# Split weights for the keys' projection, and matmul passes given first choice, in a two-layer hybrid decoder step

## The chip, the cores and the metric

The kernel runs on one core of a Trainium2 chip. The metric is the device time of one execution in microseconds (us); lower is better. Before the change the median of three runs is 1530.75 us (1529.62 to 1531.14). One execution was profiled: it took 1529.38 us, of which the profile's span covers 1527.6 us.

A core has five engines that run side by side, each through its own queue in order: TensorE (matrix products; the profile shows its matmuls as PE and its weight loads as PEld), VectorE (DVE), ScalarE (ACT), GpSimd (POOL) and SyncE (SP), which here issues the transfers. TensorE multiplies a stored 128x128 block of weights with a moving operand and adds up in a PSUM bank; there are eight banks.

## The reference

One step of a decoder trunk with two layers and 1024 features, for 256 prompt tokens and 8 sequences of 4 sample tokens, 288 columns in all. All of it is float32. Each layer adds half a SwiGLU block, a mixer, half a second SwiGLU block and a gated projection. The mixer is Mamba-2 in layer 0 and RWKV-7 in layer 1. The change concerns RWKV, cut here to what matters:

```python
u_prev = jnp.concatenate([shift0[:, None].astype(u.dtype), u[:, :-1]], axis=1)
xx = u_prev - u
mixed = u[None] + xx[None] * mu[:, None, None, :]
xr, xw, xk, xv, xa, xg = ...
r = xr @ w_r
k = xk @ w_k
v = xv @ w_v
w = -jax.nn.softplus(-(w0 + jnp.tanh(xw @ w1) @ w2)) - 0.5
a = jax.nn.sigmoid(a0 + (xa @ a1) @ a2)
g = jax.nn.sigmoid(xg @ g1) @ g2
...
S = (S * d_t[:, :, None, :] + sa[..., None] * (kk_t * a_t)[:, :, None, :]
     + v_t[..., None] * k_t[:, :, None, :])
```

w_r, w_k, w_v and the output matrix are 1024x1024: 8 by 8 tiles of 128x128.

## The kernel before, in words

Activations stand with features on the 128 partitions and the 288 tokens along the row, so a 1024-feature tensor is eight tiles of 128x288. The kernel runs eight stages in order: feed-forward, Mamba, feed-forward, gate of layer 0; feed-forward, RWKV, feed-forward, gate of layer 1.

**Products in three passes.** Most matrix products split both operands into a rounded high part, in a reduced float32 format that TensorE takes in one pass (fp32r in the profile), and a low part, the rest. `mm3` (L156) then issues three matmuls for each weight tile: high weights by high activations, high weights by low activations, low weights by high activations. All of them go through `mm` (L147), so in the profile they carry line L149. `hilo` (L162) splits an activation: a copy on ScalarE (L141) and a subtraction on VectorE (L167 or L170).

**Two streams of weights.** `Stream` loads units of eight weight tiles (512 KB) on SyncE's queue (L42). `ws` carries the weights that are split: for each four tiles ScalarE writes the high part whi (L57) and VectorE the low part wlo (L58). It splits up to 16 tiles ahead of use; its units have four buffers (`wraw`), the split parts six. `wn` carries weights used whole, in plain float32 (`next_whole`): in RWKV the first matrices of decay, a and gate (r_wa1, r_g1: 8 and 16 tiles) and w_k (64 tiles). Its first unit is loaded before the stage, into a buffer of `wraw`; when the stage begins, `k.wn.pool, k.wn.bufs = pool, 2` gives the later ones two buffers of their own (L1521). A plain float32 tile stands in the profile as two matmuls and two weight loads with raw as the weight.

**The RWKV stage.** `lead` (L1059) normalises, makes xx, mixes the gate's input and forms the sums of r_wa1 and r_g1 (the gate's sums stay in banks 2 and 3 until `gates` reads them). Then the main loop runs over p, one 128-feature block of outputs (two heads) at a time, and interleaves three things that belong to different blocks: `chain(p-2)`, the recurrence of a block, a series of small matmuls that each wait for VectorE or ScalarE and give them work in turn (solve, solved, state, then the group norm); `prep`, which makes the matrices of a block in two halves that run in two loops (it reads k, r, sw and sa, inverts triangular blocks in half precision, and uses banks 2, 3 and 7); and `fill(p)`, the projections. `fill` runs `bulk2(p-1)` (gate output g and the v projection) and `bulk(p+1)` (k and r, and `small`: the decay sw and the rate sa, one split tile each, then a sigmoid on VectorE at L1133 and on ScalarE). The projections use banks 0 and 1 in turn. In `bulk`, for p = 0 the order is k, small, r; for the later blocks it is small, k, r. Each projection is eight weight tiles, after each of which the generator hands back, so that the loop can set 1.6 of them against each step of the others. `mix` (L1115) makes xk, xv, xr with the first block: xk stays whole, xv and xr are split by `hilo`. For the last block the order of all matmuls is fixed by hand (`kept`), and in the last two loops the output matrix takes the projections' place.

**What sets the order.** The source gives a program order. A scheduler then plays all engines through in simulated time: whenever an engine is free, it issues the ready instruction that stands first, by its priority, which is its place in the program order unless the source says otherwise. So a projection's passes fill the times in which the small matmuls of `chain` and `prep` aren't ready, pass by pass if need be. The order found is fixed; on the chip each engine follows its list.

## Time and profile before

| | us |
|---|---|
| median of 3 runs | 1530.75 |
| the profiled execution | 1529.38 |
| its span | 1527.6 |
| TensorE busy: matmuls, weight loads | 1504.1, 1418.5 |
| VectorE, ScalarE busy | 1099.2, 966.1 |
| the L149 matmuls with high weights and act (5520) | 1121.7 |
| the L149 matmuls with plain weights (176 for 88 tiles) | 54.0 |
| all splits of weights: ScalarE, VectorE (754 each) | 473.5, 515.8 |

A matmul's record needs care: the next matmul starts while the record of the last is still open, so a mean duration (297 ns for a split pass) is longer than the step from start to start. The times of a stretch are therefore read from start to start. PEld is the weight loads' own row. A window gives busy times in a stretch of the span; the chain of waits follows the last instruction back to whatever released it.

### The profile page before, as it was taken

The numbers are of one execution on the slowest core, as the hardware profiler recorded it, in microseconds if no ns is written. First come the engines' busy times: TensorE is split into PE (matmuls) and PEld (weight loads), VectorE is DVE, ScalarE is ACT, GpSimd is POOL, SyncE is SP. The second block draws the span as 40 slices with busy tenths as digits, with TensorE's granted clock in tenths as the row PEclk, the third lists the DMA queues.
The fourth block names the chain that finished last, engine by engine and source line by source line (L and its number), as shares of the span: only waits on it lengthen the run. The fifth ranks groups of instructions, "written<-read, shape, count | busy, mean of one in ns | idle before, by whom it ended". The sixth has DMA issues, their size and how long they took to land.

```text
span 1527.6 us, 35589 instructions
## 1 busy us (share of the span) xinstructions
PE 1504.1 (98%) x14178; PEld 1418.5 (93%) x14178; DVE 1099.2 (72%) x2320; ACT 966.1 (63%) x2201; POOL 60.2 (4%) x162
## 2 busy tenths in 40 slices
PE   9999999999999999999999999999999999999997
PEld 9999998999999999999999999777777778999997
DVE  7666578899998666656876655897777768666666
ACT  6555458999997655554755554586666646555545
POOL 0000002112110000000000000200000000000000
PEclk9999999999999999999999999999999999999999
DMA  7555564766766555555555555622221125555552
GB/s 233 166 167 165 167 204 138 241 235 214 240 220 195 174 167 167 165 169 166 170 166 166 166 166 166 208 84 73 71 85 58 62 75 165 167 167 166 166 169 68
DMA packets 75575, 243.48 MB, mean 159 GB/s; under 512 B 11728, under 2 KB 16976, under 8 KB 75408
## 3 DMA queue, kind: packets, MB, share of 16 engines
q1 hardware_dynamic: 75408, 241.21, 49.1%
q8 instruction: 111, 1.82, 0.5%
q14 instruction: 56, 0.46, 0.1%
HBM read 226.54 MB, written 14.64 MB: 158 GB/s over the span
## 4 chain that ended last, share of the span: by engine, by line
PE 91%; DVE 4%; ACT 3%; DMA 1%; issue 1%; SPq 0%; DVEq 0%; ACTq 0%
PE bank L149 85%; PE bank L783 1%; DVE wlo L58 1%; PE bank L787 1%; PE bank L779 1%; DMA raw<-in_wn 1%; ACT whi L57 1%; PE bank L760 0%; DVE AA L1288 0%; ACT L136 0%; PE bank L818 0%; ACT seg L141 0%; DMA raw<-in_w 0%; PE bank L752 0%; ACT xc L141 0%
## 5 line engine op out<-in xcount | busy, mean ns | idle before, releaser
L149 PE MATMUL bank<-act,whi 128*128 128x288 f32 x5520 | 1121.7, 297 | 2.5 <-ACT whi L57 1.6
L149 PEld LDWEIGHTS bank<-act,whi 128*128 128x128 f32 x5520 | 885.7, 188 | 11.0 <-ACT whi L57 2.1
L149 PE MATMUL bank<-act,wlo 128*128 128x288 f32 x2760 | 812.4, 295 | 0.1
L57 ACT ACTIVATE whi<-raw 128x512 fp32r<-128x512 f32 x754 | 473.5, 632 | 445.6 <-PE bank L149 435.3
L58 DVE TENSOR_TENSOR wlo<-raw,whi 128x512 fp32r<-128x512 f32 x754 | 515.8, 689 | 270.2 <-ACT whi L57 241.9
L149 PEld LDWEIGHTS bank<-act,wlo 128*128 128x128 f32 x2760 | 520.4, 189 | 1.9 <-DVE wlo L58 0.3
L149 PE MATMUL bank<-more,whi 128*128 128x288 f32 x384 | 77.1, 295 | 0.0
L149 PEld LDWEIGHTS bank<-more,whi 128*128 128x128 f32 x384 | 61.4, 188 | 0.0
L149 PE MATMUL bank<-act,raw 128*128 128x288 f32 x176 | 54.0, 429 | 2.7 <-DVE sw L1133 1.4
L335 DVE TENSOR_TENSOR u<-bank,s 128x288 f32<-128x288 f32 x88 | 40.2, 456 | 22.8 <-PE bank L149 22.8
L149 PE MATMUL bank<-more,wlo 128*128 128x288 f32 x192 | 56.4, 294 | 0.0
L332 DVE TENSOR_TENSOR t<-bank,rstd 128x288 f32<-128x288 f32 x88 | 39.8, 456 | 22.2 <-PE bank L149 22.1
L684 DVE SCALAR_TENSOR_TENSOR conv_a<-X,vec,conv_a 128x312 f32<-128x312 f32 x96 | 51.0, 535 | 2.4 <-ACT conv_a L141 2.1
L141 ACT ACTIVATE s<-t 128x288 f32<-128x288 f32 x104 | 45.8, 443 | 6.1 <-DVE t L377 4.4
L141 ACT ACTIVATE X<-bank 128x256 f32<-128x256 f32 (+2 forms) x98 | 30.6, 343 | 16.9 <-PE bank L149 16.2
L149 PEld LDWEIGHTS bank<-act,raw 128*128 128x128 f32 x176 | 29.9, 189 | 11.2 <-DVE sw L1133 1.7
L141 ACT ACTIVATE act<-h,vec 128x288 fp32r<-128x288 f32 (+1 forms) x71 | 37.0, 527 | 4.1 <-DMA h<-in_xT 2.9
L149 PEld LDWEIGHTS bank<-more,wlo 128*128 128x128 f32 x192 | 36.2, 189 | 0.0
L136 ACT ACT_TABLE_LOAD x25 | 32.1, 1283 | 1.1 <-PEq L1761 0.7
L170 DVE SCALAR_TENSOR_TENSOR act<-h,vec,act 128x288 fp32r<-128x288 f32 x56 | 28.3, 512 | 5.6 <-ACT act L141 5.6
L181 DVE TENSOR_TENSOR ss<-ss,sq 128x288 f32<-128x288 f32 x62 | 28.0, 452 | 1.9 <-ACT sq L141 1.7
L141 ACT ACTIVATE sq<-h 128x288 f32<-128x288 f32 x63 | 26.9, 431 | 3.8 <-DVE h L381 3.7
(371 smaller groups left out, 1605.4 us busy)
## 6 DMA issues: line engine op xcount, KB each, us to landing
raw<-in_w SPq DMA_DIRECT2D x377, 512.0 KB, 3.6
h0a<-in_ssm_a SPq DMA_DIRECT2D x16, 512.0 KB, 5.8
h0b<-in_ssm_b SPq DMA_DIRECT2D x16, 512.0 KB, 5.4
out_ssm_s<-h0b SPq DMA_DIRECT2D x16, 512.0 KB, 4.4
raw<-in_wn SPq DMA_DIRECT2D x11, 512.0 KB, 4.2
S<-in_wkv_in SPq DMA_DIRECT2D x8, 256.0 KB, 3.0
out_wkv_s<-S SPq DMA_DIRECT2D x8, 256.0 KB, 2.1
h<-in_xT SPq DMA_DIRECT2D x8, 144.0 KB, 4.5
```

Of the source, the lines that this page charges most:

```text
L57: nc.scalar.activation(hi, src, AF.Copy)
L58: nc.vector.tensor_tensor(lo, src, hi.bitcast(F32), ALU.subtract)
L136: load = self.nc.scalar.preload_act_table_set(s)
L141: i = self.nc.scalar.activation(out, in_, func, **kw)
L149: i = self.nc.tensor.matmul(*a, **kw)
L170: nc.vector.scalar_tensor_tensor(lo, src, scale, hi.bitcast(F32), ALU.mult, ALU.subtract)
L181: nc.vector.tensor_tensor(self.ss, self.ss, sq, ALU.add)
L332: nc.vector.tensor_tensor(t, pg, r, ALU.mult)
L335: nc.vector.tensor_tensor(u, pu, s, ALU.mult)
L684: nc.vector.scalar_tensor_tensor(a[:, :312], X[:, t:t + 312], k.g(f"conv_w{t}")[:, ct:ct + 1], a[:, :312], ALU.mult, ALU.add)
L779: nc.tensor.matmul(pyi[q:q + 32, 128 + 4 * b:132 + 4 * b], h0a[:, b, q:q + 32], C[:, 256 + 4 * b:260 + 4 * b], start=True, stop=True)
L783: nc.tensor.matmul(py[64 * hh:64 * hh + 64, o:o + n], xdt[:n, c, 2 * j + hh], Pm[:n, hh, o:o + n], start=True, stop=True)
```

## The change

Four things are edited.

1. `mm3` issues its second and third pass inside `high_priority`, which gives them the priority of the program's start: once such a pass is ready, it goes ahead of everything else that is ready on TensorE. This holds for all stages. With `follow`, the first pass gets it as well.
2. `proj` sets `follow` for the blocks after the first (p > 0), for all tiles but the first of each four (kt % 4 > 0). So four weight tiles, twelve passes, come one after another once the first pass of the first has been issued, as far as they are ready.
3. The keys' projection goes through `mm3` too. Its 64 weight tiles move from `wn` to `ws` (288 and 24 tiles in place of 224 and 88) and are split; xk is split by `hilo` into the tiles 0 to 7 and eight new tiles xkl.
4. `small` runs between k and r for every block, not ahead of k for the later ones, and the two buffers of `wn`'s own are gone: its units after the first go to the four of `wraw`.

```diff
+    def together(self, follow):
+
+        return self.tc.high_priority() if follow else contextlib.nullcontext()
+
-    def mm3(self, ps, w, x, start, stop):
+    def mm3(self, ps, w, x, start, stop, follow=False):
         (wh, wl), (xh, xl) = w, x
-        self.mm(ps, wh, xh, start=start, stop=False)
-        self.mm(ps, wh, xl, start=False, stop=False)
-        self.mm(ps, wl, xh, start=False, stop=stop)
+        with self.together(follow):
+            self.mm(ps, wh, xh, start=start, stop=False)
+        with self.together(True):
+            self.mm(ps, wh, xl, start=False, stop=False)
+            self.mm(ps, wl, xh, start=False, stop=stop)
...
             if i == 0:
                 out[kt] = k.A[8 + kt], k.A[16 + kt]
+            elif i == 2:
+                out[kt] = k.A[kt], self.t(f"xkl{kt}", dt=F32R)
...
             if p == 0:
                 self.mix(i, kt, x)
-            if n == "k":
-                self.k.mm(ps, k.wn.next_whole("r_wk", kt, p), x[kt], start=kt == 0, stop=kt == KD - 1)
-            else:
-                k.mm3(ps, k.ws.next("r_w" + n, kt, p), x[kt], kt == 0, kt == KD - 1)
+            k.mm3(ps, k.ws.next("r_w" + n, kt, p), x[kt], kt == 0, kt == KD - 1, p > 0 and kt % 4 > 0)
...
-            k.renew(0, 8, F32)
-            k.renew(8, 16)
-            self.xk = k.A[0:8]
-            self.xv, self.xr = [[None] * KD for _ in range(2)]
+            k.renew(0, 16)
+            self.xk, self.xv, self.xr = [[None] * KD for _ in range(3)]
...
-        if p > 0:
-            yield from small()
         yield from self.proj("k", 2, self.xk, p)
-        if p == 0:
-            yield from small()
+        yield from small()
         yield from self.proj("r", 0, self.xr, p)
...
-        k.wn.pool, k.wn.bufs = pool, 2
...
-COUNT = {"ffn": 24 * KF, "ple": 80, "mamba": 520, "rwkv": 224}
-WHOLE = {"rwkv": 88}
+COUNT = {"ffn": 24 * KF, "ple": 80, "mamba": 520, "rwkv": 288}
+WHOLE = {"rwkv": 24}
```

## The prediction

> **What bounds the kernel now.** I read the page first, for the share of each engine, then the table of windows, then the chain that ended last.

> ```profile
> span 1527.6 us, 35589 instructions
> ...
> PE 1504.1 (98%) x14178; PEld 1418.5 (93%) x14178; DVE 1099.2 (72%) x2320; ACT 966.1 (63%) x2201; POOL 60.2 (4%) x162
> ...
> PEld   9999998999999999999999999777777778999997
> ```

> TensorE is the engine to ask about, and its weight loads show a dent only in slices 26 to 33, which is the RWKV stage (about 970 to 1270 us). Two windows, one of a feed-forward stage and one of an RWKV loop (start and end, length, then busy time and count of PE, PEld, DVE, ACT, POOL, the granted clock, the DMA share and GB/s):

> ```profile
> 1300.00:1350.00 50.00, 50.00 (x380) 50.00 (x380) 32.53 (x58) 26.29 (x48) 0.00 (x0) 1.00 0.52 167
> ...
> 1112.08:1143.76 31.68, 31.35 (x495) 23.65 (x493) 23.49 (x66) 21.47 (x60) 0.00 (x0) 1.00 0.27 81
> ```

> The feed-forward stage runs 380 passes in 50 us, 0.131 us each, with nothing between: a new order of passes can win nothing there, and the same holds for the gates. What the change is worth is read in the RWKV loop. Its chain:

> ```profile
> by line: PE bank L149 90.0%; DVE AA L1288 5.7%; DVE wlo L58 1.9%; DVE sa L1133 1.6%; DVE sw L1133 0.9%; DVE S L1446 0.9%; issue 0.9%
> ...
> 1142.22 0.30 DVE sw L1133
> ...
> 1142.65 0.51 DVE sa L1133
> 1143.16 0.60 DVE wlo L58
> 1143.76 0.60 DVE AA L1288
> ```

> ```profile
> 1080.40 1.21 DVE AA L1288 x2
> ...
> 1206.95 1.25 DVE AA L1288 x2
> ```

> The pair of AA masks comes back every 31.6 us (four loops from 1080.40 to 1206.95). In a loop TensorE carries the chain for nine tenths; once per loop it passes to VectorE for 2 to 3 us, where sw, sa and a weight split stand ahead of the masks.

> **The loop, part by part.** How projections and small matmuls alternate, from TensorE's timeline:

> ```profile
> 1062.03 0.31 PE L149 MATMUL bank<-Z,XT 64*64 64x64 f16 x8
> 1062.17 0.29 PE L149 MATMUL bank<-XT,Z 64*64 64x64 f16 x8
> 1062.39 0.75 PE L149 MATMUL bank<-act,raw 128*128 128x288 f32 x2
> ...
> 1114.71 0.75 PE L149 MATMUL bank<-act,raw 128*128 128x288 f32 x2
> 1115.39 0.33 PE L149 MATMUL bank<-rhs,TT 64*64 64x64 f32 x4
> ...
> 1125.74 1.24 PE L149 MATMUL bank<-act,raw 128*128 128x288 f32 x4
> 1126.91 0.33 PE L149 MATMUL bank<-rhs,TT 64*64 64x64 f32 x4
> 1127.17 0.54 PE L149 MATMUL bank<-act,whi 128*128 128x288 f32 x2
> 1127.54 0.29 PE L149 MATMUL bank<-act,wlo 128*128 128x288 f32 x1
> 1127.77 0.33 PE L149 MATMUL bank<-SAV,BKt 128*64 128x64 f32 x2
> ...
> 1142.15 0.29 PE L149 MATMUL bank<-la,wlo 128*128 128x288 f32 x1
> ```

> Start to start, a plain float32 tile (two instructions) that stands alone takes 1115.39 - 1114.71 = 0.68, a pair of them 1126.91 - 1125.74 = 1.17. A tile in three split passes that stands alone takes 1127.77 - 1127.17 = 0.60, against 3 x 0.131 = 0.39 in a long run: each run of passes pays 0.21 for its two ends. The small matmuls pay as well: eight of them take 0.14 when more small ones follow (1062.03 to 1062.17), 0.22 when a projection follows (1062.17 to 1062.39), so about 0.1 per change.

> From 1114.71 to 1142.15 the loop holds 20 runs of projection tiles: 16 plain instructions for k in six runs (four tiles alone, two pairs: 4 x 0.68 + 2 x 1.17 = 5.06) and 57 split passes (24 for v, 24 for r, 9 for g, sw and sa) in 14 runs, 9.6 us start to start by the rows between these two.

> - *k in three passes, two groups of four.* Two runs of 12 passes: 2 x (12 x 0.131 + 0.21) = 3.57 for 5.06, saved 1.5. Without grouping, eight lone tiles save only 8 x 0.08 = 0.6.
> - *v and r in groups.* 57 passes in about 6 runs: 57 x 0.131 + 6 x 0.21 = 8.7 for 9.6, saved 0.9.
> - *Fewer changes.* The small matmuls stand in 18 stretches; with these runs and the normalisations' pairs left, about 11: 7 x 0.1 = 0.7 saved.
> - *sw and sa between k and r instead of ahead of k.* They leave the VectorE stretch of the chain (0.30 + 0.51 above). The split and the masks stay: 0.8 saved. They write single buffers that the running preparation reads; later in the loop that read is longer past, so I add no wait.

> That is 3.9 us. Against it stands what the scattered tiles do now: they fill TensorE's waits for VectorE in the dependent steps. Where such a wait is bare already:

> ```profile
> PEld bank L149 <- DVE TT L1381: 3.2, 4, 0.8
> PEld bank L149 <- DVE rhs L1426: 3.0, 9, 0.7
> ```

> Seven stretches lose their filler. A bare wait costs 0.33 (3.0 over 9, the solve steps) to 0.8 (3.2 over 4), and nothing where the other two of the three interleaved sequences have matmuls ready: 0 to 5.6 us. I take half of the seven at 0.33, the row of the solve steps, which stand beside k and r: 1.2. Net 2.7 per loop, bounds -1.7 (slower) to 3.9. Six loops carry a k projection (outputs 2 to 7; 0 and 1 fall in the opening): 6 x 2.7 = 16.2. The two loops after them have v alone; half of the 0.9 + 0.7 each makes 1.6, of which I take 1, since the last steps have an order of their own. Feed-forward, Mamba and gate stages: 0, within 1 either way.

> The splits of k's weights are new work beside this: 8 tiles in a loop are two splits.

> ```profile
> L57 ACT ACTIVATE whi<-raw 128x512 fp32r<-128x512 f32 x754 | 473.5, 632 | 445.6 <-PE bank L149 435.3
> ...
> L58 DVE TENSOR_TENSOR wlo<-raw,whi 128x512 fp32r<-128x512 f32 x754 | 515.8, 689 | 270.2 <-ACT whi L57 241.9
> ...
> raw<-in_wn SPq DMA_DIRECT2D x11, 512.0 KB, 4.2
> ```

> ScalarE goes from 21.5 to 22.7 us in a loop, VectorE from 23.5 to 24.9. A loop of 29 us hides both; one of 25 would not. The weights are the same bytes on the same queue.

> **The opening, which pays.** Between the lead and the first loops VectorE is the bound:

> ```profile
> 970.00:1010.00 40.00, 35.30 (x220) 26.28 (x219) 38.02 (x99) 28.82 (x81) 10.26 (x35) 1.00 0.50 163
> ```

> ```profile
> L167 DVE TENSOR_TENSOR act<-t,act 128x288 fp32r<-128x288 f32 x8 | 3.4, 448 | 0.2 <-ACT act L141 0.2
> L58 DVE TENSOR_TENSOR wlo<-raw,whi 128x512 fp32r<-128x512 f32 x5 | 3.4, 683 | 0.1
> ```

> Splitting xk adds 8 x 0.45 = 3.6 to VectorE, and the weights of the first two k projections up to 4 x 0.68 = 2.7, so 3.6 to 6.3 with no cover (VectorE 38.0 of 40). ScalarE's share has room. Second, the gate's weights (in_wn) no longer get two buffers of their own but queue for the four that the main stream uses. SyncE, then TensorE and VectorE in that time:

> ```profile
> 974.17 0.33 SPq L42 DMA_DIRECT2D raw<-in_wn  x1
> 974.92 0.33 SPq L42 DMA_DIRECT2D raw<-in_w  x1
> 975.31 0.42 SPq L42 DMA_DIRECT2D raw<-in_wn  x1
> ...
> 988.63 0.33 SPq L42 DMA_DIRECT2D raw<-in_w  x1
> ```

> ```profile
> 981.38 5.98 PE L149 MATMUL bank<-act,raw 128*128 128x288 f32 x24
> 988.01 4.15 PE L149 MATMUL bank<-act,raw 128*128 128x288 f32 x16 [0.65 <-DMA raw<-in_wn]
> ...
> 998.53 0.29 PE L149 MATMUL bank<-ql,ones_m 128*128 128x288 f32 x1
> ```

> ```profile
> 987.88 0.68 DVE L58 TENSOR_TENSOR wlo<-raw,whi 128x512 fp32r<-128x512 f32 x1
> ```

> The load at 974.92 takes the buffer that the first gate unit leaves; the next buffer comes free with the split that ends at 988.56, and the load follows at 988.63. In the changed kernel the second unit of gate weights stands at that place and lands 4.2 later, at 993. The third needs one more unit split, which needs passes of k done: after eight mixes and half of their splits, about 996.5, landed at 1000.7. Its eight tiles take 16 x 0.248 = 4.0 (4.15 less the last 0.43, over 15), to 1004.7, where the last gate matmul now ends at 987.4. Behind it waits the first preparation, whose norm goes into a bank that the gate's sum holds: done about 1006 where it is now at 998.8, so 7 late. On SyncE a load that waits holds up what is queued behind it, here the constants and the states; they are needed only after that norm, so I price nothing for them. VectorE has its 3.6 to 6.3 to do in that time, so the two are not added: 7, bounds 3.6 (the loads come in time) and 10 (part of the VectorE work comes after the wait).

> **Sum.** -16.2 - 1 + 7 = -10.2. The profiled execution took 1529.38 (span 1527.6), so 1519.2; the median of the runs, 1530.75, lies 1.4 above it, so 1520.5.

> **Rivals.** *Slower: the dependent steps set the loop's length.* PEld is busy for 23.65 of 31.68 us, no more than VectorE with 23.49, so TensorE may be held by waits that short fillers happen to cover. A run of 12 passes is 1.78 long where a tile alone is 0.60 or 0.68; a step that comes ready just behind its start is up to 1.1 later, six times a loop, and the seven bare waits follow. From 3.9 us of these the loop gains nothing (seven waits at 0.56, between the two rows), and the opening's 7 us remain: 1537.8; with waits at 0.8 it is 10 us more. Against it speaks the chain, nine tenths TensorE, with PE idle for 0.33 us. [...] Chance 0.24.

> *The order hardly groups.* The priorities only act where an instruction is ready when its engine is free in the planned order; if splits come late there, the tiles stay scattered. Then a loop gains 8 x 0.08 for k and half of sw and sa's 0.8, 1.0, six loops 6, against 7: 1531.8, no change. Chance 0.13.

> *All of it.* The waits stay covered (3.9 a loop) and the opening costs VectorE's 3.6 alone: -23.4 - 1 + 3.6 = -20.8, 1510. Chance 0.17.

> **How the numbers follow.** My forecast has 0.46; between net gains of 1.6 and 3.4 per loop and 4 to 10 us of opening it reaches from 1513 to 1530, nearly all of it below 1527.7. A difference under 0.2%, 3 us, can't be told from none here. Faster: 0.46 + 0.17 = 0.63. Same: 0.13. Slower: 0.24. The range leaves out the slower half of the first rival (0.12) and less than half of the last (0.07): 1509 to 1538.

> **What would show it.** Right: the AA pair returns every 28 to 30 us; whi and wlo rows of 12 passes without small matmuls between; PE idle per loop up from 0.33 to about 1.5; VectorE near 25 a loop; the last gate matmul near 1004 and the first ql norm near 1006. Wrong: a period of 31 us or more with TensorE waiting for rhs, SAV or Z (first rival); passes still three by three (second); gate weights issued before 985 (the opening is cheaper); or a feed-forward window with fewer than 378 passes in 50 us, which no step here foresees.

## The result and the profile after

The changed kernel takes 1565.45 us (median of four runs, 1563.89 to 1566.72) where the kernel before takes 1530.86 beside it: a ratio of 1.0227 (95% interval 1.0209 to 1.0245), 34.6 us slower. The forecast was 1520.5 with a range up to 1538. The profiled execution took 1563.89.

The page of the changed kernel, with lines moved by one (L150 is the matmul, L58 and L59 the splits of weights):

```profile
span 1562.1 us, 35769 instructions
...
PE 1518.1 (97%) x14242; PEld 1444.5 (92%) x14242; DVE 1113.4 (71%) x2344; ACT 979.3 (63%) x2225; POOL 60.5 (4%) x162
...
PEclk9999999999999999999999999879999879999999
```

The same row on the page of before:

```profile
PEclk9999999999999999999999999999999999999999
```

Two things stand there. TensorE's rows are busy for 14 us more while the span grew by 34.5, so it is idle for 44.0 us where it was idle for 23.5. And the granted clock, nine tenths or more in every slice before, falls below nine tenths in two places of the RWKV stage.

For what follows I cut the stage into four parts, by the same marks in every kernel: from the first plain matmul of the lead to the first AA masks (the opening), two loops, five steady loops, and the last part up to the last group norm. First before, then after (columns as in the prediction's windows):

```profile
969.60:1007.31 37.71, 33.63 (x188) 24.74 (x188) 35.72 (x92) 26.55 (x75) 10.26 (x35) 1.00 0.49 157
1007.31:1048.08 40.77, 39.59 (x639) 32.03 (x640) 34.05 (x93) 31.60 (x82) 0.00 (x0) 1.00 0.24 84
1048.08:1206.91 158.83, 157.33 (x2440) 119.50 (x2439) 118.98 (x329) 109.35 (x302) 0.00 (x0) 1.00 0.24 72
1206.91:1272.95 66.04, 62.01 (x872) 48.62 (x868) 43.86 (x117) 32.32 (x87) 0.00 (x0) 0.97 0.24 74
```

```profile
968.21:1014.15 45.94, 39.66 (x221) 30.55 (x223) 40.99 (x104) 32.44 (x87) 9.85 (x35) 0.89 0.35 110
1014.15:1067.19 53.04, 48.72 (x660) 40.86 (x658) 37.63 (x98) 35.52 (x90) 0.00 (x0) 0.81 0.22 70
1067.19:1234.19 167.00, 155.39 (x2463) 127.59 (x2460) 125.96 (x338) 114.16 (x308) 0.00 (x0) 0.94 0.24 76
1234.19:1307.19 73.00, 63.52 (x859) 51.23 (x860) 43.14 (x116) 31.10 (x85) 0.00 (x0) 0.85 0.18 59
```

All four parts are longer: 8.2, 12.3, 8.2 and 7.0 us, 35.7 together. What lies behind them is the same (254.6 us before, 254.9 after), and the feed-forward window still holds 380 passes:

```profile
1335.00:1385.00 50.00, 50.00 (x380) 50.00 (x379) 32.39 (x58) 26.27 (x49) 0.00 (x0) 1.00 0.53 169
```

The last column but two is the clock. Length times what it lacks to 1.00, summed over the parts, is 36.1 us after (5.1, 10.1, 10.0, 11.0) and 2.0 before: 34 us more. Length less PE busy, the idle time, is 31.7 after and 10.8 before: 21 more. The two make 55 and the parts grew by 35.7, so at most some 19 us of TensorE's work went away (an estimate, and an upper one: what the clock lacks is taken as lost wholly; two pairs of kernels below lost two thirds to nine tenths of it). That is the kind of work the forecast wanted to save, and more than twice as much was lost in its place.

Where the loops lose it shows in TensorE's timeline of one steady loop (start, length of the stretch, operation; in brackets idle time and who ended it):

```profile
1149.98 0.33 PE L150 MATMUL bank<-rhs,TT 64*64 64x64 f32 x4
...
1152.78 1.10 PE L150 MATMUL bank<-AR,S 64*64 64x8 f32 x32
1153.82 0.40 PE L150 MATMUL bank<-ch,ones_m 128*128 128x288 f32 x1
1155.18 0.40 PE L150 MATMUL bank<-cl,ones_m 128*128 128x288 f32 x1 [0.96 <-DVE cl L1217]
...
1156.17 0.33 PE L150 MATMUL bank<-SAV,AA 64*64 64x64 f32 x4 [0.23 <-ACT s L142]
...
1157.28 0.68 PE L150 MATMUL bank<-act,whi 128*128 128x288 f32 x2
...
1158.00 0.68 PE L150 MATMUL bank<-act,whi 128*128 128x288 f32 x2
...
1160.77 0.43 PE L150 MATMUL bank<-act,whi 128*128 128x288 f32 x2
...
1161.16 0.42 PE L150 MATMUL bank<-act,whi 128*128 128x288 f32 x2
```

From 1148 on TensorE runs dependent steps, with only the small projections' passes (gate and decay) between them and no projection tile of v, k or r. It waits 0.96 for VectorE with nothing to put there. Then the tiles come, all at once, in groups of twelve passes, but a tile now takes 0.72 (1157.28 to 1158.00), where it takes 0.39 once the clock is full again (1160.77 to 1161.16). In windows of two microseconds:

```profile
1150.00:1152.00 2.00, 1.80 (x31) 1.39 (x30) 1.49 (x6) 1.43 (x6) 0.00 (x0) 1.00 0.34 131
1152.00:1154.00 2.00, 1.99 (x36) 1.57 (x36) 1.36 (x6) 1.88 (x7) 0.00 (x0) 1.00 0.49 128
1154.00:1156.00 2.00, 0.98 (x3) 0.37 (x2) 2.00 (x6) 1.11 (x3) 0.00 (x0) 1.00 0.09 32
1156.00:1158.00 2.00, 1.83 (x10) 1.76 (x11) 1.24 (x4) 1.94 (x6) 0.00 (x0) 0.63 0.00 0
1158.00:1160.00 2.00, 2.00 (x9) 1.77 (x8) 0.91 (x2) 0.90 (x4) 0.00 (x0) 0.52 0.00 0
...
1030.00:1032.00 2.00, 1.14 (x22) 0.86 (x18) 1.50 (x4) 1.83 (x5) 0.00 (x0) 1.00 0.05 12
1032.00:1034.00 2.00, 1.58 (x17) 1.02 (x11) 2.00 (x7) 0.83 (x2) 0.00 (x0) 0.91 0.00 0
...
1042.00:1044.00 2.00, 2.00 (x29) 1.54 (x26) 0.00 (x0) 1.10 (x3) 0.00 (x0) 0.50 0.00 0
...
1050.00:1052.00 2.00, 2.00 (x14) 1.83 (x16) 1.04 (x2) 1.05 (x4) 0.00 (x0) 0.83 0.10 41
```

TensorE is idle for 1.02 of two microseconds (1154 to 1156), and the clock granted next is one half, for 3.41 us from 1156.51. In the second loop it is idle for 0.86 and 0.42 of two (1030 to 1034), and the clock is one half for 17.07 us from 1033.63. In this stage the changed kernel has ten stretches at half clock: five of 3.41 us, one of 6.83, three of 10.24 and one of 17.07. TensorE's single waits are shorter than any of these: none between 1150 and 1156 is longer than 0.97 and none in the stage longer than 1.5, and in the 3.41 us ahead of 1156.51 PE is busy for 2.22.

Idle time isn't the whole of it either. The kernel before halves its clock once in this stage, from 1227.36 to 1230.77, and by its records PE is busy for 6.77 of the 6.83 us ahead of that, with small matmuls and projections mixed:

```profile
1221.00:1226.00 5.00, 4.95 (x89) 3.79 (x88) 2.95 (x9) 2.56 (x10) 0.00 (x0) 1.00 0.67 214
1226.00:1231.00 5.00, 5.00 (x65) 3.92 (x60) 1.84 (x5) 2.94 (x7) 0.00 (x0) 0.66 0.02 6
```

And behind 998.66 to 1002.08, where PE is busy for only 2.00 of 3.42 us, the kernel before keeps its 1.00. So scattered idle time stands ahead of most drops here (in the changed kernel 0.51 to 1.88 us of the 3.41 ahead of nine of the ten, 0.21 ahead of the tenth, at 1187.23); that it is what brings them is not shown.

### The profile page after: what moved, and what is told of

It is laid out like the page before. It is cut to its first block, busy times and chain, and to the rows that moved or that the text cites. A ratio compares the mean times of both kernels' runs of the same rounds, so it can differ in the third digit from the quotient of the medians.

```text
span 1562.1 us, 35769 instructions
## 1 busy us (share of the span) xinstructions
PE 1518.1 (97%) x14242; PEld 1444.5 (92%) x14242; DVE 1113.4 (71%) x2344; ACT 979.3 (63%) x2225; POOL 60.5 (4%) x162
## 4 chain that ended last, share of the span: by engine, by line
PE 87%; DVE 6%; ACT 5%; issue 1%; DMA 1%; POOL 0%; SPq 0%; DVEq 0%; ACTq 0%
PE bank L150 82%; ACT whi L58 1%; DVE wlo L59 1%; PE bank L790 1%; PE bank L786 1%; PE bank L794 1%; ACT seg L142 1%; PE bank L767 0%; ACT s L142 0%; ACT sa L142 0%; PE bank L759 0%; DMA raw<-in_w 0%; ACT X L142 0%; DMA raw<-in_wn 0%; ACT ch L142 0%
## 5 line engine op out<-in xcount | busy, mean ns | idle before, releaser
L150 PE MATMUL bank<-act,whi 128*128 128x288 f32 x5584 | 1144.9, 299 | 7.4 <-ACT act L142 2.8
L150 PEld LDWEIGHTS bank<-act,whi 128*128 128x128 f32 x5584 | 904.4, 190 | 18.8 <-ACT act L142 4.4
L150 PE MATMUL bank<-act,wlo 128*128 128x288 f32 x2824 | 833.4, 296 | 0.1
L58 ACT ACTIVATE whi<-raw 128x512 fp32r<-128x512 f32 x770 | 483.0, 632 | 459.3 <-PE bank L150 447.6
L59 DVE TENSOR_TENSOR wlo<-raw,whi 128x512 fp32r<-128x512 f32 x770 | 526.2, 689 | 282.7 <-ACT whi L58 257.4
L150 PEld LDWEIGHTS bank<-act,wlo 128*128 128x128 f32 x2824 | 537.6, 191 | 0.5 <-DVE wlo L59 0.4
L150 PE MATMUL bank<-more,whi 128*128 128x288 f32 x384 | 77.1, 295 | 0.0
L150 PEld LDWEIGHTS bank<-more,whi 128*128 128x128 f32 x384 | 61.4, 188 | 0.0
L150 PE MATMUL bank<-more,wlo 128*128 128x288 f32 x192 | 56.4, 294 | 0.0
L150 PEld LDWEIGHTS bank<-more,wlo 128*128 128x128 f32 x192 | 36.2, 189 | 0.0
L174 DVE TENSOR_TENSOR act<-u,act 128x288 fp32r<-128x288 f32 x64 | 28.9, 451 | 0.0
L142 ACT ACTIVATE seg<-bank,na 128x128 f32<-128x128 f32 (+1 forms) x96 | 25.4, 362 | 5.2 <-PE bank L661 5.1
## 6 DMA issues: line engine op xcount, KB each, us to landing
raw<-in_w SPq DMA_DIRECT2D x385, 512.0 KB, 3.5
h0a<-in_ssm_a SPq DMA_DIRECT2D x16, 512.0 KB, 5.5
h0b<-in_ssm_b SPq DMA_DIRECT2D x16, 512.0 KB, 5.5
out_ssm_s<-h0b SPq DMA_DIRECT2D x16, 512.0 KB, 3.9
raw<-in_wn SPq DMA_DIRECT2D x3, 512.0 KB, 3.5
```

The lines of the kernel that those rows point to most:

```text
L58: nc.scalar.activation(hi, src, AF.Copy)
L59: nc.vector.tensor_tensor(lo, src, hi.bitcast(F32), ALU.subtract)
L142: i = self.nc.scalar.activation(out, in_, func, **kw)
L150: i = self.nc.tensor.matmul(*a, **kw)
L174: nc.vector.tensor_tensor(lo, src, hi.bitcast(F32), ALU.subtract)
```

## The experiments

"Over before" is a kernel's median less that of the kernel before in the same comparison; the parts come from each kernel's profile, by the marks above, with the clock of the two middle parts.

| kernel | over before, us | opening | two loops (clock) | five loops (clock) | last part |
|---|---|---|---|---|---|
| before | 0 | 37.7 | 40.8 (1.00) | 158.8 (1.00) | 66.0 |
| after | 34.6 | 45.9 | 53.0 (0.81) | 167.0 (0.94) | 73.0 |
| e1_passes | 1.5 | 39.7 | 41.2 (1.00) | 156.2 (1.00) | 69.7 |
| e2_groups | 6.4 | 37.4 | 45.7 (0.96) | 157.0 (0.98) | 72.2 |
| e3_keys | 7.0 | 43.7 | 44.2 (0.88) | 159.2 (1.00) | 66.1 |
| e4_nogroups | 18.9 | 45.0 | 47.8 (0.82) | 159.3 (1.00) | 73.2 |
| e5_kfill | 24.8 | 46.2 | 51.6 (0.83) | 162.1 (0.97) | 72.1 |
| e6_warm | 41.8 | 46.5 | 50.8 (0.83) | 171.6 (1.00) | 77.1 |
| e7_gatesfirst | 34.9 | 45.9 | 53.4 (0.78) | 166.8 (0.94) | 73.0 |
| e8_projpasses | -2.4 | 38.3 | 41.2 (1.00) | 156.5 (1.00) | 69.0 |
| e9_gates | 29.2 | 45.9 | 46.6 (0.96) | 170.2 (0.91) | 73.9 |
| e10_warm1 | 32.3 | 46.9 | 52.7 (0.77) | 166.0 (0.99) | 74.5 |
| e11_steps | 30.1 | 46.5 | 59.1 (0.83) | 161.2 (0.99) | 68.4 |
| e12_small | 6.5 | 38.9 | 42.2 (0.96) | 160.3 (1.00) | 67.5 |
| e13_oldsmall | 17.1 | 44.9 | 44.0 (1.00) | 161.2 (0.92) | 73.0 |
| e14_keysonly | 4.1 | 44.5 | 41.8 (1.00) | 156.5 (1.00) | 67.0 |
| e15_keyspasses | 1.3 | 43.9 | 40.6 (1.00) | 154.1 (1.00) | 65.2 |
| e16_keysgroups | 19.7 | 44.4 | 44.3 (1.00) | 167.8 (0.88) | 68.2 |
| e17_pool | 7.7 | 47.1 | 44.1 (1.00) | 152.7 (1.00) | 66.8 |
| e18_poolgates | 6.1 | 50.4 | 44.0 (0.96) | 153.8 (1.00) | 65.2 |

**The parts of the change, each way.** The kernel before with the first choice for a tile's second and third pass, everywhere; then with the groups of four tiles as well:

```diff
+        with self.together(True):
+            self.mm(ps, wh, xl, start=False, stop=False)
+            self.mm(ps, wl, xh, start=False, stop=stop)
```

> The kernel before, with the second and third pass of every split product given first choice and nothing else changed. If the runs of twelve passes do the harm, this stays near the kernel before: 1528 to 1534 us, clock 0.99 or more. If the passes' first choice alone breaks the order that hides the dependent steps, it is 1540 us or more. If the opening does it (the gate's weights and xk's split), this is unchanged at 1531.

```diff
-                k.mm3(ps, k.ws.next("r_w" + n, kt, p), x[kt], kt == 0, kt == KD - 1)
+                k.mm3(ps, k.ws.next("r_w" + n, kt, p), x[kt], kt == 0, kt == KD - 1, p > 0 and kt % 4 > 0)
```

> The kernel before with the passes' first choice and the groups of four for v and r; the keys stay in plain float32, the small projections ahead of k, the gate's weights in their own buffers. If the runs of twelve passes do the harm (dependent steps late, TensorE idle, clock down), most of the 35 us is here: 1545 to 1560, clock under 0.99. If the opening does it, 1525 to 1533. If it needs the keys in three passes, near 1531 too.

Passes alone: 1532.73, ratio 1.0012 (1.0001 to 1.0024). Groups added: 1537.59, ratio 1.0043 (1.0027 to 1.0058), 4.9 slower than passes alone, in the same comparison. That is neither the 1545 to 1560 set for harm by the groups nor the 1533 at most set for none. In the five steady loops:

```profile
1051.79:1208.80 157.01, 151.55 (x2441) 117.34 (x2438) 117.51 (x326) 108.33 (x297) 0.00 (x0) 0.98 0.22 70
```

TensorE's busy time fell from 157.3 to 151.6 us, with v and r alone in groups, and the loops by 1.8: two thirds of the saved work came back as idle time, and the two loops ahead and the last part grew by 5.0 and 6.2. Beside passes alone even these loops are 0.9 longer, with 5.5 us of idle time in place of 0.8.

The changed kernel without passes and groups (split keys, shared buffers, sw and sa moved), then without the groups alone, then with groups for v and r but not for k:

```diff
-        with self.together(True):
+        with self.together(False):
...
-            k.mm3(ps, k.ws.next("r_w" + n, kt, p), x[kt], kt == 0, kt == KD - 1, p > 0 and kt % 4 > 0)
+            k.mm3(ps, k.ws.next("r_w" + n, kt, p), x[kt], kt == 0, kt == KD - 1)
```

> The changed kernel with no priority anywhere: the keys in three passes, the small projections after k, the gate's weights in the shared buffers. If the runs of twelve do the harm, only the opening's 7 us and small gains in the loops are left: 1530 to 1538. If the opening starts the harm (a late first preparation, then waits at half clock), it is 1550 or more, and the AA masks of the third block stand near 1067 as in the changed kernel and not near 1048.

```diff
-            k.mm3(ps, k.ws.next("r_w" + n, kt, p), x[kt], kt == 0, kt == KD - 1, p > 0 and kt % 4 > 0)
+            k.mm3(ps, k.ws.next("r_w" + n, kt, p), x[kt], kt == 0, kt == KD - 1)
```

> The changed kernel without the groups: passes two and three keep first choice, the first pass of each tile has its own place. If the groups do the harm: 1530 to 1540. If the passes' first choice does: within 5 us of 1565. If the opening does: 1550 or more, as without any priority.

```diff
-            k.mm3(ps, k.ws.next("r_w" + n, kt, p), x[kt], kt == 0, kt == KD - 1, p > 0 and kt % 4 > 0)
+            k.mm3(ps, k.ws.next("r_w" + n, kt, p), x[kt], kt == 0, kt == KD - 1, n != "k" and p > 0 and kt % 4 > 0)
```

> The changed kernel with groups for v and r alone: k's tiles keep first choice for passes two and three but stand where the program order has them. If TensorE's waits became bare because no projection tile is left to fill them, the five steady loops (167.0 us between the AA masks of the third and the eighth block) fall to 157 to 160 and the time to 1550 to 1556. If three passes for k are the harm by their splits on VectorE and ScalarE, the loops stay at 165 or more.

1538.19, 1550.15 and 1555.70: each further step of the new order costs more, though in the kernel before passes cost 1.5 and groups 4.9. The parts don't add up. With groups for v and r but not for k the kernel is still 9.8 better than the whole change, which fits k's scattered tiles being worth more as fillers than their ends cost. Its five loops, 162.1, fall between the marks set for that (157 to 160) and for harm by k's splits (165 or more).

**Is the clock a cause or a sign?** The changed kernel with matmuls of 128 columns on constants, into columns that nobody reads, ahead of each step of the recurrence, three of them and then one:

```diff
+        def warm(ps):
+
+            for _ in range(WARMERS if k.kept is None else 0):
+                k.mm(ps[:, 128:256], self.ones_m, self.ones_m, start=True, stop=True)
...
+            warm(pr)
```

> The changed kernel with three more matmuls of 128 columns on constants ahead of every step of the recurrence (solve, solved, state), into columns of its bank that nothing reads; about 330 in all, some 20 to 30 us of TensorE work that does nothing but keep TensorE busy. If the loss is the lower granted clock that follows idle time, the clock of the span rises from 0.975 to 0.985 or more and the time falls in spite of the work: 1545 to 1562. If the waits themselves are the loss and the clock costs nothing, it is the added work: 1572 to 1590.

> The changed kernel with one matmul of 128 columns on constants, into columns of the bank that nobody reads, ahead of each solve and state step (about 16 more per loop, some 1.7 us of TensorE each loop). Clock theory: the five steady loops stand at a granted clock of 0.98 or more and get shorter although work was added, the time is 1545 to 1560. Rival (only the waits themselves cost, the clock is a sign of them): nothing is won and the added work is paid, 1568 to 1575.

1572.64 and 1564.74. The five loops, with three and with one:

```profile
1066.47:1238.06 171.59, 167.70 (x2683) 145.26 (x2682) 126.42 (x339) 114.07 (x309) 0.00 (x0) 1.00 0.22 70
```

```profile
1068.42:1234.43 166.01, 159.11 (x2542) 133.94 (x2537) 127.40 (x342) 115.64 (x312) 0.00 (x0) 0.99 0.25 79
```

One added matmul per step, 79 in these loops, brings the clock from 0.94 to 0.99, and the loops get 1.0 shorter although work was added (the loops of e7_gatesfirst, with the changed kernel's order and clock, lie 0.2 from its). Three bring it to 1.00, but their own work is more than the clock gives. With one, the idle time falls as well, from 11.6 to 6.9 us, so these kernels by themselves don't part the clock from the waits. Nor do the added matmuls hold the clock everywhere: with one per step the last part has 2.3 us of idle time in place of 9.5, and its clock is 0.86 in place of 0.85. In the whole kernel neither paid; 1564.74 lies between the two theories.

Two pairs on record part them. In the five steady loops the changed kernel and e9_gates run the same 2456 matmuls (by their starts) in the same order, and in the last part e15_keyspasses and e17_pool run the same 866; the three kernels are described below. The steady loops of e9, then the last part of e15 and of e17:

```profile
1061.01:1231.18 170.17, 158.62 (x2463) 130.78 (x2460) 126.04 (x338) 114.64 (x308) 0.00 (x0) 0.91 0.24 75
```

```profile
1208.29:1273.52 65.23, 60.61 (x873) 47.69 (x871) 44.55 (x120) 32.44 (x87) 0.00 (x0) 1.00 0.25 81
```

```profile
1214.36:1281.12 66.76, 62.14 (x873) 49.20 (x870) 44.49 (x119) 32.42 (x87) 0.00 (x0) 0.97 0.25 81
```

The idle time is the same within each pair (11.6 and 11.6, 4.6 and 4.6). e9 spends 29.2 us at half clock where the changed kernel spends 19.7, and takes 3.2 longer. e17 keeps step with e15, within 0.03 us from matmul to matmul, up to 1273.82, has half clock for 3.41 us, and is 1.5 behind from there on. So the clock costs time by itself: two thirds to nine tenths of the half that it withholds. And with order and idle time equal, something else decided here whether it fell; what, wasn't tried.

**Does a step wait behind a group, or is nothing left to fill?** In the changed kernel, the recurrence's own matmuls get the first choice too:

```diff
+                    k.first = q is steps
                     if next(q, "end") == "end":
                         gens.remove(q)
+                    k.first = False
...
-        i = self.nc.tensor.matmul(*a, **kw)
+        with self.together(self.first):
+            i = self.nc.tensor.matmul(*a, **kw)
```

> The changed kernel in which the matmuls of the dependent recurrence steps get the scheduler's first choice as well, so that they are not queued behind groups of twelve passes. If the groups cost because a step that comes ready behind a group's start waits for its end: the five steady loops take under 160 us together (167.0 in the changed kernel), their clock is 0.98 or more, the time is 1545 to 1555. If the idle time comes because the fillers are used up and nothing is left for TensorE in the steps' waits: the loops stay at 165 to 169 us and the time within 4 us of 1565.

1562.54. The five loops shorten by 5.8 us to 161.2, just above the mark set, their clock rises to 0.99, and the groups break up: 6 runs of twelve passes in these loops where the changed kernel has 23. But the two loops ahead take 6.0 more, with 694 matmuls in them for 660. Undecided as a whole; for the steady loops it speaks for the groups as the cause, since the loops recover as far as the groups dissolve.

**The place of sw and sa.** Moved alone, in the kernel before; then put back, in the changed kernel:

```diff
-        if p > 0:
-            yield from small()
         yield from self.proj("k", 2, self.xk, p)
-        if p == 0:
-            yield from small()
+        yield from small()
```

> The kernel before with one thing moved: the small projections (sw, sa and the gate's) stand between k and r in every loop instead of ahead of k. The forecast had 0.8 us for this in each of six loops: 1526 to 1529 if that was right. If the masks are then held by something else that comes last, or the small projections come late for the steps that read them: 1530 to 1534.

> The changed kernel with one thing put back: sw and sa stand ahead of k again in the loops. Moving them alone had made the kernel before 6.5 us slower. If that place is a cause of its own: 1557 to 1561, the steady loops shorter by about 1.5 us. If it is the same loss met twice (idle time that any change of the order brings): within 3 us of 1565.

1538.91, ratio 1.0046 (1.0029 to 1.0062), and 1548.10, ratio 1.0110. The step that was to give 0.8 per loop costs 6.5 by itself and 17.5 in the changed kernel (34.6 less 17.1), half of its loss. Five steady loops with sw and sa moved alone, then with them put back:

```profile
1054.61:1214.93 160.32, 157.06 (x2460) 119.73 (x2459) 121.26 (x331) 109.22 (x303) 0.00 (x0) 1.00 0.24 72
```

```profile
1057.36:1218.57 161.21, 150.33 (x2477) 126.42 (x2474) 124.89 (x336) 112.22 (x305) 0.00 (x0) 0.92 0.25 78
```

Of the 6.5, the four parts account for 5.6 (1.2, 1.4, 1.5, 1.5), spread over all of the stage. In the steady loops, at a clock of 1.00, it is idle time, 3.3 us in place of 1.5; where those waits start wasn't followed further. Between e14_keysonly and e3_keys, which differ in this move alone, it costs 2.9. With sw and sa put back the clock of the two loops behind the opening is 1.00 again (0.81 in the changed kernel), and that part gives back 9.1 of the 17.5. The steady loops are still at 0.92.

**The keys alone, then step by step.** The kernel before with the split keys and the shared buffers only; with the first choice for second and third pass in the RWKV projections only; with the groups as well (the first edit, in part, against the kernel before, each later one against the one ahead of it):

```diff
-                k.mm3(ps, k.ws.next("r_w" + n, kt, p), x[kt], kt == 0, kt == KD - 1)
+            k.mm3(ps, k.ws.next("r_w" + n, kt, p), x[kt], kt == 0, kt == KD - 1)
...
-        k.wn.pool, k.wn.bufs = pool, 2
```

> The kernel before with the split keys and the shared buffers of weights alone; sw and sa in their old place, nothing with the scheduler's first choice. With sw and sa moved as well it took 1538.2; moving them alone cost 6.5. If the parts add up: about 1532, the opening later by 6 to 7 us and the steady loops shorter by about 1 us each. If the opening's loss is all that counts: 1537 to 1539.

```diff
-    def mm3(self, ps, w, x, start, stop, follow=False):
+    def mm3(self, ps, w, x, start, stop, follow=None):
...
-        with self.together(False):
+        with self.together(follow is not None):
...
-            k.mm3(ps, k.ws.next("r_w" + n, kt, p), x[kt], kt == 0, kt == KD - 1)
+            k.mm3(ps, k.ws.next("r_w" + n, kt, p), x[kt], kt == 0, kt == KD - 1, False)
```

> The kernel before with the split keys, sw and sa in their old place, and second and third pass of a tile with the first choice in the RWKV projections alone; no groups. First choice there alone had given 3.7 us in the kernel before. If it does the same for the keys' tiles, which stand in three passes here: the loops give 9 us, the opening takes 6 to 7, 1525 to 1529. If idle time eats it: 1533 to 1540.

```diff
-            k.mm3(ps, k.ws.next("r_w" + n, kt, p), x[kt], kt == 0, kt == KD - 1, False)
+            k.mm3(ps, k.ws.next("r_w" + n, kt, p), x[kt], kt == 0, kt == KD - 1, p > 0 and kt % 4 > 0)
```

> The same with groups of four tiles. If the groups are what brings idle time and the half clock behind it: 8 to 20 us above the kernel without them, the clock of the steady loops below 0.98. If groups are harmless once sw and sa stand where they stood: within 4 us of it.

1535.10 (1.0022, 1.0006 to 1.0037), 1532.30 (1.0005, 0.9991 to 1.0019) and 1550.71 (1.0127). The first two lie between the marks set for them. The groups alone, with all else equal, cost 18.4 us, 13.7 of it in the steady loops, first without, then with groups:

```profile
1054.15:1208.29 154.14, 152.21 (x2479) 123.20 (x2478) 123.91 (x336) 115.04 (x312) 0.00 (x0) 1.00 0.25 79
```

```profile
1058.24:1226.08 167.84, 157.22 (x2477) 131.75 (x2474) 125.50 (x336) 112.48 (x305) 0.00 (x0) 0.88 0.24 76
```

The same work (2479 and 2477 matmuls); idle time goes from 1.9 to 10.6 us, and the clock of 0.88 lacks 20.1 us of full speed (167.84 x 0.12). Together that is 28.8 for loops that are 13.7 longer: by this estimate the groups save TensorE at most some 15 us of work here, and lose about twice as much. This pair is the clearest of the study. TensorE's matmuls wait in it for the group norm's rstd (3.5 us with groups), for g, the gate's output (3.1), and for AR, a matrix of the preparation (2.1), where without groups their longest entry is 1.0 for AA. Without groups the split keys do what they should: five loops in 156.5 with the keys alone and 154.1 with the first choice, against 158.8, so 0.5 and 0.9 per loop. That buys nothing in the end, since the opening takes 6.2 more.

The first choice for the RWKV projections' passes without the keys:

```diff
+    def mm3(self, ps, w, x, start, stop, follow=None):
...
+        with self.together(follow is not None):
+            self.mm(ps, wh, xl, start=False, stop=False)
+            self.mm(ps, wl, xh, start=False, stop=stop)
...
+                k.mm3(ps, k.ws.next("r_w" + n, kt, p), x[kt], kt == 0, kt == KD - 1, False)
```

> The kernel before with first choice for passes two and three in RWKV's v and r projections alone, not in the output matrix, the small projections or the other stages. With first choice everywhere the steady loops won 2.6 us and the last part lost 3.7. If the last part's loss comes from the output matrix's passes, only the win is left: 1526 to 1529. If it comes from the order that the loops leave behind, 1531 to 1534.

1528.44 in ten runs (1525.17 to 1535.19) beside 1530.86: ratio 0.9976 (0.9963 to 0.9989). It is the only kernel of the study that is faster than both, by 2.4 us, with its own runs spread over ten. Its profile is of the longest of its ten runs and can't show where it wins.

**The opening.** The gate's weights loaded first, by two loads ahead of the stage; then inside the products of the stage before:

```diff
+    for _ in range(2):
+        k.wn.load()
     k.sh = k.st([P, KD, 8], name="sh")
```

> The changed kernel with the second and third unit of the gate's weights loaded ahead of the main stream's last prefetches, so that they take the first two buffers that come free. If the late gate weights make the opening long, the first AA mask comes 4 to 6 us earlier after the first plain matmul (45.9 us in the changed kernel, 37.7 before) and the next two blocks run at a higher clock: 1545 to 1558. If xk's split alone makes the opening long, within 3 us of the changed kernel.

```diff
                     self.nc.sync.dma_start(self.spill[m], t)
+                    if m == 1:
+                        self.wn.load()
+                        self.wn.load()
```

> The changed kernel with the second and third unit of gate weights loaded ahead of the last weights of the main stream (inside the products of the first stage) instead of behind them. Theory (after idle time TensorE is granted half its clock, so late gate weights cost their wait and then the clock of the stretch behind it): the stretch from the lead to the first masks falls from 45.9 to about 41 us, its clock rises above 0.95, the next one falls from 53.0 to 45 to 50, and the time is 1550 to 1560. Rival (the opening is set by the splits on VectorE, the loads only show there): both stretches stay within 1 us and the time within 3 us of 1565.

The first edit left the loads in their places (the second unit of gate weights is loaded at 985.45 where the changed kernel loads it at 985.52) and so tells nothing of the opening; 1565.72. The second moved them: 1561.61, ratio 1.0191. In the changed kernel TensorE runs the gate's sums and the first norm at

```profile
990.11 5.31 PE L150 MATMUL bank<-act,raw 128*128 128x288 f32 x16
...
1000.09 4.04 PE L150 MATMUL bank<-act,raw 128*128 128x288 f32 x16
...
1005.69 0.29 PE L150 MATMUL bank<-ql,ones_m 128*128 128x288 f32 x1
```

and with the loads moved, the last of them at

```profile
981.87 5.29 PE L150 MATMUL bank<-act,raw 128*128 128x288 f32 x20 [0.52 <-DVE act L1129]
```

The gate is done 17 us earlier (its last pair ended at 1004.1, here at 987.2), and the opening is as long as it was, 45.9, as the rival had it. The two loops behind it take 46.6 at a clock of 0.96 in place of 53.0 at 0.81, as the theory had it. What is late in the opening instead:

```profile
998.00:1006.00 8.00, 5.00 (x26) 3.57 (x24) 7.96 (x22) 7.66 (x21) 0.00 (x0) 0.88 0.14 43
1006.00:1014.45 8.45, 7.64 (x77) 6.96 (x78) 5.34 (x14) 4.88 (x12) 0.00 (x0) 0.51 0.26 93
```

VectorE is busy for 7.96 of 8 us while TensorE idles for 3.0, and then the clock is half. So VectorE with the splits may be a second limit of the opening, of the same length as the late gate weights. Taking VectorE's share of xk's split to GpSimd, first alone, then with the loads moved as above:

```diff
-            nc.vector.tensor_tensor(lo, src, hi.bitcast(F32), ALU.subtract)
+            (eng or nc.vector).tensor_tensor(lo, src, hi.bitcast(F32), ALU.subtract)
...
-            k.hilo(*out[kt], m)
+            k.hilo(*out[kt], m, eng=self.nc.gpsimd if i == 2 else None)
```

> The split keys with sw and sa in their old place and first choice for the second and third pass (no change against the kernel before), and the subtraction of xk's split (8 in the opening, 0.45 us each on VectorE) on GpSimd. If VectorE sets the opening: from the lead to the first masks 43.9 falls to about 41 us, the time to about 1528. If the late gate weights set it: within 1 us of 43.9 and 3 us of the time without it.

> The same with the second and third unit of gate weights loaded ahead of the last weights of the main stream as well. Theory (the opening has two limits of about the same length, the gate weights and VectorE's splits, so that taking away one shows nothing): with both away the lead comes to the first masks in 38 to 40 us, as before the change, and the time is 1522 to 1527. Rival (the wait for main weights that now come late takes their place): 43 to 45 us, the time at 1530 to 1534.

1538.68 (1.0059) and 1537.09 (1.0036): both misses. The opening grows to 47.1 and 50.4. GpSimd's rows and the waits on them, without the loads moved:

```profile
L174 POOL TENSOR_TENSOR xkl<-t,act 128x288 fp32r<-128x288 f32 x8 | 6.6, 836 | 3.5 <-ACT act L142 3.5
```

```profile
PEld bank L150 <- POOL xkl L174: 7.2, 4, 5.5
...
DVE t L1126 <- POOL xkl L174: 4.3, 3, 2.7
```

A subtraction takes 836 ns there against 453 on VectorE (the same eight, without the move), and mix, copy and subtraction of a tile follow one another: TensorE waits 5.5 for one of them, and VectorE waits for the buffer of the mix. A slower engine made the chain of the opening longer, whatever load it took off VectorE. Whether VectorE is a second limit, and whether the opening has room at all for the split keys, stays open.

## Why the prediction was wrong, point by point

- *What bounds the kernel.* Right for the stages it read: the feed-forward window holds its 380 passes. In the loop it read nine tenths of the chain on TensorE as the mark of an engine whose work sets the time. It missed that the work was also cover.
- *The ends of runs.* Right. It had the projections' tiles at 14.7 us a loop before and 12.3 after (5.06 + 9.6, and 3.57 + 8.7). From start to start they take 15.0 in the steady loops of before, 13.7 in the changed kernel at a clock of 0.94, and 12.5 and 11.3 where one and three added matmuls keep the clock up. 23 of the 45 runs in the changed kernel's five loops are of twelve passes and 7 of thirteen or fourteen, so the order did group. The 0.7 for fewer changes was not measured by itself.
- *k in three passes.* 1.5 per loop with groups was never seen as time; 0.6 without them was forecast and 0.5 measured (0.9 with the first choice, which gave 0.5 without the split keys).
- *sw and sa: the second step that failed.* Wrong in sign: 0.8 saved per loop was taken, and moving them alone costs 6.5 us, 17.5 in company. The chain shows what ended last in one execution, not what would be last after a move; "I add no wait" rested on the read of single buffers alone.
- *Bare waits: the step that failed.* "1.2, bounds 0 to 5.6" counted seven waits at the length of the wait. TensorE's idle time rose by 2.0 us per steady loop (11.6 less 1.5, over five), so the waits themselves were within the bounds. What had no term is the granted clock: what it lacks comes to 10 us in the five loops, 10 in the two loops ahead, 11 in the last part, 5 in the opening, beside 2 in all before, and the two pairs of equal order lost two thirds to nine tenths of such an amount as time. The trace of before showed a clock of 1.00 in every steady loop, and the forecast had nothing for a change of it, though the last part of before stands at 0.97. What brings the clock down stays open in part: the order with groups does in the one pair that differs in it alone (1.00 and 0.88), but idle time is not the whole of it.
- *The last part.* 1 us of gain was taken; it takes 7.0 more, at a clock of 0.85.
- *The opening.* The steps came out on their marks: last gate matmul forecast at 1004.7, ended at 1004.1; first norm at 1006, begun at 1005.7; first masks 7 late, 6.8 late. Part of that agreement is luck. The second unit of gate weights was issued at 985.5 and not 988.6, its sixteen matmuls took 5.31 us with the clock at one half until 992.67, and with the gate weights early the opening is as long. VectorE's work, which the forecast didn't add, may be a second limit of the same length; the two runs on that were misses.
- *The marks.* Masks every 28 to 30 us were forecast. They come from 1067.19 to 1234.19 in five loops, 33.4 each:

```profile
1067.19 1.28 DVE L1289 TENSOR_TENSOR AA<-bank,r_const 128x512 f32<-128x512 f32 x2
...
1234.19 1.29 DVE L1289 TENSOR_TENSOR AA<-bank,r_const 128x512 f32<-128x512 f32 x2 [1.50 <-PE bank L150]
```

 VectorE was to be near 25 us a loop: 25.2. PE idle was to be about 1.5: 2.3.
- *The slower rival.* It had the right side, and its kind of wait only in part. TensorE's matmuls waited for SAV 1.0 us and for rhs 0.6 in the stage before, and for Z not at all; in the changed kernel

```profile
PE bank L150 <- DVE SAV L1433: 2.6, 5, 0.5
PE bank L150 <- DVE Z L1344: 2.2, 5, 0.6
...
PE bank L150 <- DVE rhs L1427: 1.5, 4, 0.5
```

 That is 4.7 of the 21 us of new idle time; the rest is spread over norms, masks, the gate and the opening. The rival ran short too: with its highest price, 0.8 a wait, it reached 1548, because it too priced waits without the clock. And it held that the loop's length is dependence, so that denser passes could gain nothing: with the split keys and the first choice, without groups, the loops do shorten, to 30.8 us. PEld's busy time, which the rival sets beside VectorE's, doesn't tell the orders apart: it is 0.80 of the steady loops without groups and 0.78 with them (123.20 of 154.14, 131.75 of 167.84), and they differ by 13.7 us.

## What to carry to other kernels

When TensorE's fillers are made denser, ask what will stand in the waits they leave: by the rows of before grouping saves 0.21 us for each run of passes that it joins to another (0.60 for a tile alone, 0.39 in a long run), and with all else equal it cost 18.4 us here. Give the granted clock a term of its own, since a clock of 1.00 before a change is no promise for after it (1.00 and 0.94 in the five steady loops); read it in windows of two microseconds, and price 3.41 us at half clock at some 1.5 us, as the last parts of e15 and e17 show it. Try the parts of such a change one at a time, and in company, where a move that costs 6.5 us alone cost 17.5: here the first choice for second and third passes in the RWKV projections alone was the one part that gained.
